# A hybrid decoder block on one Trainium2 core: small products of all lanes at every fourth step of the stream

## The chip, the cores and the metric

The kernel runs on one core of one Trainium2 chip. The metric is the device time of one execution in microseconds, as the median of several executions. Lower is better.

## The reference

One decoder layer for 512 tokens of width 2048 in float32, with an adaLN conditioning vector `c`. Cut to what matters:

```python
sh1, sc1, g1, sh2, sc2, g2 = split(silu(c) @ w_ada + b_ada)
h = rmsnorm(x, norm1_g) * (1 + sc1) + sh1
p = h @ w_in                                  # one projection, columns split
# A: convolution group: GLU, causal depthwise convolution of width 31, group norm, silu
u = p_val * sigmoid(p_gate);  u = conv31(u, conv_w) + conv_b
A = silu(group_norm(u, 16 groups))
# B: RWKV-7 group, 16 heads of 64: token shift, decay, a state update for every token
q = token_shift(p_rwkv);  r, k, v, xw, xa, xg = split(q)
S = S * w_t + (S a_t) b_t^T + v_t k_t^T;  y_t = S r_t
B = (group_norm(y) + bonus * v) * g           # bonus = sum(r * k * r_k)
x = x + g1 * (concat[A, B] @ w_out)
h = rmsnorm(x, norm2_g) * (1 + sc2) + sh2
x = x + g2 * ((silu(h @ w_ff1) * (h @ w_ff3)) @ w_ff2)
return rmsnorm(x, norm_f_g)
```

The output is (1, 512, 2048).

## The kernel before

Every large product runs as three products of split operands (`mm3`: high by high, high by low, low by high), 128 rows by 512 columns. After a head that projects the first columns, a **stream** (`stream`) walks over units of 16 steps; one step is one `mm3`. `in_units` are the projections in `ORDER`: k, v, r of pair 1, then for each pair of heads five units of 16 steps (val, gate of an earlier pair, k, v, r of the next), 592 steps in all. `out_units` are the output projection; its first 48 steps are the last ones beside which the lanes run, before `open_ff` at step 640 finishes what is left. While a step's products run, `emit` prepares the next weights: ScalarE copies the high part (line 92), VectorE subtracts for the low part (line 93).

Beside the stream run four **lanes** (class `Lane`). A lane has a queue of jobs, each a Python generator whose parts end at `yield`; the main loop calls `run` of every lane once after each step of the stream, and a list of numbers says how many steps the lane waits after each part.

- `pre` (`rwkv_pre`, 27 parts, one job per pair of heads): the decay and the keys (parts 1 to 6, with wide float32 products against `l1` and `bo`), the mask product `mp` (part 7), `vp` (8), `k` and `r` (8 to 10), the bonus product `bon` (11, its input is line 617), `npp` (12), two sets of transposes (13, 14), two `Q` products (15, 16), `nvp` (17), then the inverse of a triangular matrix. `inverse` takes the 16x16 diagonal blocks through DRAM to 64 lanes, where VectorE inverts them in 30 small operations (lines 701 and 704, spread over parts 12 to 16), brings them back through DRAM, and GpSimd spreads them (line 719, part 18); products follow in parts 19 to 23 (each with a VectorE or ScalarE read, line 736 among them), and parts 24 and 25 apply the inverse.
- `scan` (`rwkv_scan`, 20 parts): for each of eight chunks of 64 tokens a first half (64x64 products of the state, then `FV` on VectorE) and a second half (128x64 products, the new state), a chain of 16 parts; then a group norm (lines 812, 813, 818) and the split for the output projection.
- `cnv` (`conv`, 19 parts): 31 taps in 15 parts on VectorE (line 843), then a group norm with two wide products. Its input tile has one buffer: the convolution of the next pair needs the last one to be done (`cnv.finish` in `conv_gate`).
- `ada` (21 parts): 16 VectorE sums over loaded weights (line 882) and a product. Job 7 makes the gate row that `add_row` multiplies with the output projection's first sums; where it isn't there, `add_row` runs the lanes until it is.

The narrow products (64x64, 128x64, 64x128, 32x32) of the lanes are float32, eight to 32 instructions a part. PSUM has eight banks: three accumulators, `gg` (which the inverse's products and the mask product use), `yy` and `fp` for the scan, and two `bk` for everything that `aux` hands out. The tile framework orders each engine's queue and sets the waits.

Of the kernel before, what the change touches and what calls it, by code (L numbers as in the profile page):

```python
# [22 lines left out]
NB = CW // P  # L23
# [12 lines left out]
class Block:  # L36
    def __init__(self, ctx, tc, ins, out):
        self.ctx, self.tc, self.nc = ctx, tc, tc.nc
        self.i = ins
        self.out = out  # L40
        e = ctx.enter_context
        self.const = e(tc.tile_pool(name="const", bufs=1))
        self.act = e(tc.tile_pool(name="act", bufs=1))
        self.ps = e(tc.tile_pool(name="ps", bufs=1, space=PSUM))
        self.dram = e(tc.tile_pool(name="spill", bufs=1, space=DRAM))
# [170 lines left out]
    def fn(self, out, in_, func, **kw):  # L216
        name = self.SETS[func]
        nc, tc = self.nc, self.tc
        with ExitStack() as st:
            if self.last_fn is not None:  # L220
                st.enter_context(tc.issue_after(self.last_fn))
            if name != self.table:
                self.last_fn = nc.scalar.preload_act_table_set(name).ins
                self.table = name
            with tc.issue_after(self.last_fn):
                self.last_fn = nc.scalar.activation(out=out, in_=in_, func=func, **kw).ins  # L226
# [722 lines left out]
    def run(self):  # L949
# [20 lines left out]
        first = self.head()  # L970
# [6 lines left out]
        pres = []  # L977
        adas = [(3 + b // 4, b % 4, (sh2, s2)[b // 4], self.ada_cols) for b in range(8)]
        late = adas[8 - LATE:]
        adas = adas[:8 - LATE] + [(2, 0, None, self.ada_rows)]  # L980
        for n, ps in zip("rkv", first):
# [4 lines left out]
        pres.append((0, dict(self.rkv)))  # L986
        self.gate = {}
        ada = lambda part, cc, out, fn: fn(part, cc, out)
        self.scan, self.pre, self.cnv = Lane(self.scans, self.rwkv_scan, SCAN), Lane(pres, self.rwkv_pre, PRE, PRE0), \
            Lane(self.convs, self.conv, CONV)  # L990
        lanes = self.lanes = [self.scan, self.pre, self.cnv, Lane(adas, ada, ADA)]


        def in_units():
            last = ORDER[-1]
            for kind, b in ORDER:
                base = {"r": RWKV0, "k": RWKV0 + CW, "v": RWKV0 + 2 * CW, "val": 0, "gate": CW}[kind] + b * P

                def done(ps, kind=kind, b=b):
                    if kind in "rkv":  # L1000
                        self.rwkv_in(b, kind, ps)
                        if kind == "r":
                            pres.append((b, dict(self.rkv)))
                    elif kind == "val":
                        self.conv_val(b, ps)
                    else:
                        self.conv_gate(b, ps)
                stepped = None
                if (kind, b) == last:
                    def stepped(j):  # L1010
                        self.free += 1
                        self.mix_back(1)
                yield self.col_unit(i["w_in"][0], base, self.xh, self.xl, done, None, stepped)
# [35 lines left out]
        def out_units():  # L1049
            for cc in range(4):  # L1050
                accs = []
                for n, ks in enumerate(OUT_ORDER):
                    before = {(0, 3): open_ff, (1, 0): open_rows, (1, 1): lambda: load_x(1), (2, 0): lambda: load_x(2),
                              (3, 0): lambda: load_x(3)}.get((cc, n))
                    u = self.row_unit(
                        i["w_out"][0], ks, cc, self.mh, self.ml, accs, n == 0, n == 3,
                        self.add_row(2, cc, lambda t, cc=cc: self.x1[cc][:, t], rstd_rows),
                        before, (cc, n) == (3, 3))
                    if (cc, n) == (3, 3):
                        u.emit = {3: 1}  # L1060
                    yield u
# [272 lines left out]
        def units():  # L1334
            yield from in_units()
            yield from out_units()
            yield from fast_units()
            yield from ff2_units()

        for _ in self.stream(units()):  # L1340
            for l in lanes:
                l.run()

# [6 lines left out]

SCAN = (2, 2, 2, 3, 1, 1, 2, 3, 1, 1, 3, 2, 2, 2, 2, 2, 2, 1, 3, 2, 2)
PRE = (2, 2, 2, 2, 2, 2, 2, 2, 2, 2, 1, 2, 2, 2, 2, 3, 2, 8, 4, 2, 2, 2, 2, 1, 2, 2, 2, 1, 2)
CONV = (2, 2, 2, 2, 1, 2, 1, 2, 3, 3, 2, 2, 2, 2, 2, 2, 2, 3)
ADA = (4, 4, 4, 4, 4, 4, 4, 4, 4, 4, 4, 4, 4, 4, 4, 4, 4, 4, 6, 3, 3, 3)
ADA_ROWS = (2, 1, 2, 2, 2, 2, 2, 2, 3, 2, 3, 2, 2, 2, 2, 3, 2, 2, 4, 4, 2, 2)
PRE0 = PRE[:17] + (20,) + PRE[18:]  # L1360
LATE = 1
# [4 lines left out]
class Lane:  # L1366


    def __init__(self, queue, fn, waits, first=None):
        self.queue, self.fn, self.waits, self.first = queue, fn, waits, first or waits  # L1370
        self.job, self.n, self.wait, self.done = None, 0, 0, 0

    @property
    def busy(self):
        return bool(self.job or self.queue)

    def run(self):
        if self.wait:
            self.wait -= 1
        else:  # L1380
            next(self)

    def finish(self, n):

        while self.done < n:
            next(self)
# [129 lines left out]
```

## Time and profile before

| | us |
|---|---|
| median of 3 runs | 2484.78 (2482.81 to 2487.75) |
| the profiled execution | 2477.18 |
| its span, first to last instruction | 2475.5 |
| TensorE busy | 2373.9 (96%) |
| VectorE busy | 1784.8 (72%) |
| ScalarE busy | 1048.3 (42%) |
| mean granted TensorE clock | 0.984 |

Times in the profile are microseconds from the first instruction. PE is TensorE's products, PEld its weight loads, DVE is VectorE, ACT is ScalarE, POOL is GpSimd, SP is SyncE, which issues most transfers. A matmul's end is modelled, so what a product costs is read from the starts of the products around it. A float32 product is two instructions, a transpose and a stream product one. The stream's step 656 would start at about 931 us.

### The profile page before, as it was taken

What the parts mean: (1) busy time and instruction counts of PE and PEld (TensorE: products, weight loads), DVE (VectorE), ACT (ScalarE), POOL (GpSimd) and SP (SyncE); (2) the same over time, 40 slices, a digit from 0 to 9 for tenths busy, and PEclk for the clock granted to TensorE, in tenths of its full rate; (3) what the DMA queues carried; (4) which work ended last, traced back from release to release, by engine and by line L of the source; (5) the groups of instructions that cost most, each with busy time, mean ns of one, the idle gap of its engine ahead of it and who ended that gap; (6) DMA issues with size and microseconds to landing.
All of it is one profiled execution on the core that took longest, in us unless ns stands there. A gap on an engine that the chain in (4) does not pass through costs nothing. (4 is left out here: it accounts for less than half of the span.)

```text
span 2475.5 us, 36145 instructions
## 1 busy us (share of the span) xinstructions
PE 2373.9 (96%) x13984; PEld 1864.0 (75%) x13984; DVE 1784.8 (72%) x2727; ACT 1048.3 (42%) x1521; POOL 137.3 (6%) x232
## 2 busy tenths in 40 slices
PE   5998999999999998989999999999999999999998
PEld 4766667767766676767888888888888878888886
DVE  4764888888888885679878777787777867534434
ACT  4253464464454443246544444444444432222223
POOL 2000100100100100000000000000000000000000
PEclk9999999999999998999999999999999999999999
DMA  9953245344354458756777777767777886423332
GB/s 335 346 174 94 74 124 144 92 134 127 88 147 114 124 175 281 246 193 197 254 254 216 235 238 239 232 206 232 239 234 241 297 285 228 145 97 118 98 102 102
DMA packets 339372, 464.30 MB, mean 188 GB/s; under 512 B 42979, under 2 KB 165073, under 8 KB 338176
## 3 DMA queue, kind: packets, MB, share of 16 engines
q1 hardware_dynamic: 331312, 436.64, 56.7%
q0 software_dynamic: 7888, 25.36, 2.7%
q8 instruction: 109, 1.79, 0.3%
q14 instruction: 63, 0.52, 0.1%
HBM read 431.52 MB, written 30.41 MB: 187 GB/s over the span
## 5 line engine op out<-in xcount | busy, mean ns | idle before, releaser
L92 ACT CAST wh<-ws 128x512 fp32r<-128x512 f32 (+1 forms) x696 | 547.7, 810 | 888.8 <-PE acc L74 310.8
L93 DVE TENSOR_TENSOR wl<-ws,wh 128x512 fp32r<-128x512 f32 (+1 forms) x696 | 642.2, 938 | 364.9 <-ACT wh L92 360.5
L74 PE MATMUL acc<-xh,wh 128*128 128x512 f32 x592 | 258.7, 437 | 2.8 <-ACT wh L92 2.8
L74 PE MATMUL acc<-xl,wh 128*128 128x512 f32 x592 | 241.9, 409 | 0.0
L74 PE MATMUL acc<-xh,wl 128*128 128x512 f32 x592 | 238.6, 403 | 0.0
L882 DVE SCALAR_TENSOR_TENSOR ada<-wa,sc,ada 128x512 f32<-128x512 f32 x256 | 192.4, 752 | 63.6 <-DMA wa<-in_w_ada_dram 53.2
L74 PE MATMUL b<-wh,xh 128*128 128x512 f32 x560 | 222.1, 397 | 0.7 <-ACT ada L895 0.7
L74 PE MATMUL acc<-wh,xh 128*128 128x512 f32 x552 | 221.7, 402 | 0.0
L74 PE MATMUL acc<-wh,xl 128*128 128x512 f32 x552 | 219.7, 398 | 0.0
L74 PE MATMUL b<-wl,xh 128*128 128x512 f32 x560 | 219.6, 392 | 0.0
L74 PE MATMUL b<-wh,xl 128*128 128x512 f32 x560 | 219.1, 391 | 0.0
L74 PE MATMUL acc<-wl,xh 128*128 128x512 f32 x552 | 218.4, 396 | 0.0
L1453 DVE TENSOR_TENSOR ws<-ws,ws 128x1024 f32<-128x1024 f32 x123 | 149.7, 1217 | 0.0
L74 PEld LDWEIGHTS acc<-xh,wh 128*128 128x128 f32 x592 | 111.9, 189 | 35.6 <-issue 5.3
L74 PE MATMUL b<-wh,x 128*128 128x512 f32 x352 | 136.9, 389 | 1.4 <-ACT wh L92 1.4
L74 PE MATMUL b<-wl,x 128*128 128x512 f32 x352 | 137.0, 389 | 0.0
L74 PE MATMUL b<-wh,raw 128*128 128x512 f32 x352 | 137.0, 389 | 0.0
L74 PEld LDWEIGHTS acc<-xh,wl 128*128 128x128 f32 x592 | 112.5, 190 | 27.2 <-issue 2.2
L74 PEld LDWEIGHTS acc<-xl,wh 128*128 128x128 f32 x592 | 112.6, 190 | 24.5 <-issue 5.8
L74 PEld LDWEIGHTS b<-wh,xh 128*128 128x128 f32 x560 | 105.6, 189 | 24.1 <-ACT ada L895 2.2
L74 PEld LDWEIGHTS acc<-wl,xh 128*128 128x128 f32 x552 | 105.2, 190 | 23.8 <-DVE wl L93 2.3
L74 PEld LDWEIGHTS b<-wh,xl 128*128 128x128 f32 x560 | 105.8, 189 | 22.6 <-issue 0.5
(415 smaller groups left out, 4221.1 us busy)
## 6 DMA issues: line engine op xcount, KB each, us to landing
ws<-in_w_ff_dram SPq DMA_DIRECT2D x440, 512.0 KB, 4.8
wa<-in_w_ada_dram SPq DMA_DIRECT2D x256, 256.0 KB, 3.7
ws<-in_w_in_dram SPq DMA_DIRECT2D x74, 512.0 KB, 3.9
wa<-in_w_ada_dram SPq DMA_DIRECT2D x32, 1024.0 KB, 11.9
ws<-in_w_out_dram SPq DMA_DIRECT2D x24, 512.0 KB, 5.2
rawd<-wa POOLq DMA_DIRECT2D x28, 256.0 KB, 4.9
hr<-rawd POOLq DMA_DIRECT2D x7, 1024.0 KB, 6.3
hidd<-wa POOLq DMA_DIRECT2D x24, 256.0 KB, 5.3
```

Of the source, the lines that this page charges most:

```text
L74: return self.nc.tensor.matmul(out, lhsT=lhsT, rhs=rhs, start=start, stop=stop, skip_group_check=True)
L92: self.nc.scalar.copy(out=hi, in_=x)
L93: return self.nc.vector.tensor_tensor(out=lo, in0=x, in1=hi.bitcast(F32), op=ALU.subtract).ins
L882: nc.vector.scalar_tensor_tensor(out=acc, in0=was[r], scalar=self.sc[:, r:r + 1], in1=acc, op0=ALU.mult, op1=ALU.add)
L1453: k.nc.vector.tensor_tensor(out=out, in0=a, in1=b, op=ALU.subtract)
```

## The change

The main loop now tells each lane how many PSUM banks are free for small products at this step: two at every fourth step of the stream (`SLOT`), -1 at the others. While the first or the last pair is in preparation it is every second step. Each lane has a table (`SCAN_BANKS`, `PRE_BANKS`, `CONV_BANKS`, and `{20: 1}` for `ada`) with the banks that a part with small products takes; such a part (0 banks for those in `gg`, `fp` and `yy`) runs only where that many are left, in the order scan, pre, cnv, ada. A wait of 0 lets the lane go on with its next part at the same step. The lists of waits are new: the scan asks for every slot, so that a pair's chunks run beside the next pair's preparation; `PRE` puts parts 7 and 8, 12 and 13, 14 and 15, 16 and 17, 24 and 25 together and waits eight steps, where it was four, between GpSimd's spreading (part 18) and the inverse's products; convolutions wait three steps after each part, two at the end.

```diff
-        self.scan, self.pre, self.cnv = Lane(self.scans, self.rwkv_scan, SCAN), Lane(pres, self.rwkv_pre, PRE, PRE0), \
-            Lane(self.convs, self.conv, CONV)
-        lanes = self.lanes = [self.scan, self.pre, self.cnv, Lane(adas, ada, ADA)]
+        self.scan, self.pre, self.cnv = Lane(self.scans, self.rwkv_scan, SCAN, None, SCAN_BANKS), \
+            Lane(pres, self.rwkv_pre, PRE, PRE0, PRE_BANKS), Lane(self.convs, self.conv, CONV, None, CONV_BANKS)
+        lanes = self.lanes = [self.scan, self.pre, self.cnv, Lane(adas, ada, ADA, None, {20: 1})]
...
-        for _ in self.stream(units()):
+        for n, _ in enumerate(self.stream(units())):
+
+            ends = self.pre.done + bool(self.pre.job) in (1, NB)
+            if ends and self.pre.done:
+                self.cnv.waits = self.cnv.first = CONV_END
+            free = 2 if self.rowp is not None or n % (2 if ends else SLOT) == 0 else -1
             for l in lanes:
-                l.run()
+                free = l.run(free)
...
-SCAN = (2, 2, 2, 3, 1, 1, 2, 3, 1, 1, 3, 2, 2, 2, 2, 2, 2, 1, 3, 2, 2)
-PRE = (2, 2, 2, 2, 2, 2, 2, 2, 2, 2, 1, 2, 2, 2, 2, 3, 2, 8, 4, 2, 2, 2, 2, 1, 2, 2, 2, 1, 2)
-CONV = (2, 2, 2, 2, 1, 2, 1, 2, 3, 3, 2, 2, 2, 2, 2, 2, 2, 3)
+SLOT = 4
+SCAN = (1, 1, 1, 1, 1, 1, 1, 1, 1, 1, 1, 1, 1, 1, 1, 1, 2)
+PRE = (2, 2, 2, 2, 2, 2, 2, 0, 1, 1, 1, 6, 0, 2, 0, 2, 0, 8, 8, 2, 2, 2, 2, 2, 0, 1)
+CONV, CONV_END = (3,), (2,)
+
+SCAN_BANKS = dict.fromkeys(range(1, 16), 0) | {17: 1, 18: 1}
+PRE_BANKS = {1: 2, 2: 1, 7: 0, 8: 1, 11: 1, 12: 1, 13: 1, 14: 1, 15: 1, 16: 1, 17: 1} | dict.fromkeys(range(19, 24), 0) \
+    | {24: 1, 25: 1}
+CONV_BANKS = {16: 1, 17: 1}
 ADA = (4, 4, 4, 4, 4, 4, 4, 4, 4, 4, 4, 4, 4, 4, 4, 4, 4, 4, 6, 3, 3, 3)
...
-    def __init__(self, queue, fn, waits, first=None):
-        self.queue, self.fn, self.waits, self.first = queue, fn, waits, first or waits
+    def __init__(self, queue, fn, waits, first=None, banks={}):
+
+        self.queue, self.fn, self.waits, self.first, self.banks = queue, fn, waits, first or waits, banks
...
-    def run(self):
+    def run(self, free):
+
         if self.wait:
             self.wait -= 1
-        else:
+            return free
+        while True:
+            need = self.banks.get(self.n if self.job else 0)
+            if need is not None:
+                if need > free:
+                    return free
+                free -= need
             next(self)
+            if not self.job or self.wait >= 0:
+                self.wait = max(self.wait, 0)
+                return free
```

## Rows read from the trace of the kernel before

**Rows 1.** Windows: length, then each engine's busy time and instructions, granted clock, DMA.

```profile
233.00:833.00 600.00, 580.68 (x5225) 413.51 (x5219) 507.07 (x967) 308.86 (x467) 63.27 (x77) 1.00 0.41 115
931.00:941.00 10.00, 4.62 (x10) 1.34 (x8) 6.06 (x10) 6.56 (x9) 0.00 (x0) 0.78 0.87 286
```

**Rows 2.** TensorE's timeline around one set: start, busy, engine, line, out<-in, shape, count.

```profile
175.15 0.39 PE L74 MATMUL acc<-xh,wl 128*128 128x512 f32 x1
175.47 1.15 PE L74 MATMUL bk<-cen,v 64*64 64x64 f32 x32
176.55 0.50 PE L74 MATMUL acc<-xh,wh 128*128 128x512 f32 x1
176.89 0.39 PE L74 MATMUL acc<-xl,wh 128*128 128x512 f32 x1
```

**Rows 3.** TensorE's timeline around two sets side by side, 677 to 680 us.

```profile
676.84 0.40 PE L74 MATMUL acc<-xh,wh 128*128 128x512 f32 x1
677.08 0.39 PE L74 MATMUL acc<-xl,wh 128*128 128x512 f32 x1
...
679.45 0.50 PE L74 MATMUL acc<-xh,wl 128*128 128x512 f32 x1
679.79 0.39 PE L74 MATMUL acc<-xh,wh 128*128 128x512 f32 x1
```

**Rows 4.** TensorE's timeline, the last narrow products of the stage.

```profile
908.36 0.33 PE L74 MATMUL yy<-Q,FV 128*64 128x64 f32 x2
```

**Rows 5.** TensorE's timeline around one second half of a scan step.

```profile
694.42 0.40 PE L74 MATMUL acc<-xh,wl 128*128 128x512 f32 x1
694.74 0.33 PE L74 MATMUL yy<-Q,FV 128*64 128x64 f32 x2
695.00 0.49 PE L74 MATMUL acc<-xh,wh 128*128 128x512 f32 x1
695.42 0.34 PE L74 MATMUL fp<-FV,bkT 128*64 128x64 f32 x4
```

**Rows 6.** TensorE's timeline where two tile shapes adjoin, 322 to 325 us.

```profile
322.28 0.40 PE L74 MATMUL acc<-xl,wh 128*128 128x512 f32 x1
...
324.61 0.33 PE L74 MATMUL fp<-FV,bkT 128*64 128x64 f32 x2
324.87 0.50 PE L74 MATMUL acc<-xh,wl 128*128 128x512 f32 x1
325.21 0.40 PE L74 MATMUL acc<-xh,wh 128*128 128x512 f32 x1
```

**Rows 7.** Timeline of TensorE and VectorE at the end of the stage.

```profile
938.15 2.07 PE L74 MATMUL bk<-ada,ones 128*128 128x512 f32 x2 [3.28 <-DVE ada L882]
...
937.34 0.75 DVE L882 SCALAR_TENSOR_TENSOR ada<-wa,sc,ada 128x512 f32<-128x512 f32 x1 [1.23 <-DMA wa<-in_w_ada_dram]
938.01 0.74 DVE L859 SCALAR_TENSOR_TENSOR cy<-cy,colB,cu 128x512 f32<-128x512 f32 x1
```

**Rows 8.** TensorE's waits, 172 to 931 us: who for whom, us, times, longest.

```profile
PE bk L74 <- DVE r L617: 11.6, 7, 2.3
PE gg L74 <- POOL a L719: 8.3, 3, 5.7
PE gg L74 <- DVE a L736: 6.5, 5, 2.4
```

**Rows 9.** Timeline of VectorE and GpSimd between a mask product and a bonus product.

```profile
532.08 0.68 DVE L597 TENSOR_TENSOR kn<-gg,gm 128x512 f32<-128x512 f32 x1
...
533.34 1.76 DVE L93 TENSOR_TENSOR wl<-ws,wh 128x512 fp32r<-128x512 f32 x1
535.03 1.78 DVE L602 TENSOR_TENSOR k<-k,a 128x512 f32<-128x512 f32 x1
...
539.61 0.74 DVE L617 SCALAR_TENSOR_TENSOR r<-r,colB,k 128x512 f32<-128x512 f32 x1
...
532.91 1.65 POOL L682 TENSOR_TENSOR e<-kn,bd 128x512 f32<-128x512 f32 x1 [6.17 <-DVE kn L597]
```

**Rows 10.** Window after that bonus product.

```profile
540.60:544.00 3.40, 3.40 (x7) 1.82 (x6) 1.82 (x8) 0.00 (x0) 0.00 (x0) 0.50 0.61 193
```

## The prediction

> **What bounds the kernel now.** I read the windows by stage first [rows 1]. The stream's steps beside which the three large lanes run (640), and the 16 after them, end at about 931 us; in the long middle, 233 to 833 us, TensorE is busy 580.7 of 600 us and VectorE 507.1 (84.5%), so TensorE sets the pace and VectorE has 15% to spare. Between 931 and 941 us TensorE works 4.6 us only: it waits at the end of this stage. What follows has no lane left but the `ada` one, and the change leaves it alone.
>
> Then TensorE's own timeline. Two stream products next to each other start 0.23 us apart. One step of the preparation with 16 narrow products (32 instructions, 64x64) stretches the way from the stream product before it to the second one after it from 0.46 to 1.74 us [rows 2]: it costs 1.28 us. Two such steps that stand together, 64 instructions, cost 2.71 - 0.46 = 2.25 us [rows 3], not 2.56. So 32 instructions cost 0.97 us and 0.31 us is the price of going into narrow products and back, whatever their number. That price is what the change is about.
>
> I counted the stretches of narrow products along this timeline from 172 to 931 us: 250, the first in [rows 2], the last in [rows 4]; in 11 places a stretch changes its tile shape inside. 250 x 0.31 = 78 us of this stage go into and out of narrow products.
>
> **What moves.** No instruction is added or removed: the same products, vector operations and transfers, in another order. I stepped through the stream's loop with the old and the new lists (only the code is needed). Old: 240 lane steps with narrow products at 238 different steps of the stream. New: at 161, since each lane now waits for every fourth step (every second one for the first and last pair), and the preparation does two of its parts there at once (7 and 8, 12 and 13, 14 and 15, 16 and 17, 24 and 25). Inside these 161 stretches neighbours of the same shape meet 41 times and of another shape 38 times (a scan step's 128x64 beside the preparation's 64x64, the transposes' 64x128). Wide float32 products (the 512-column ones of `bo`, `cen`, `l1`, `l2`) run in the stream's own shape and are counted as a break; merging them is put at nothing.
>
> The trace's 250 is more than the code's 238, because the framework orders each engine's queue itself: second halves of scan steps are cut in two, two instructions, a stream product, then the rest [rows 5]. The first piece alone costs 0.58 - 0.23 = 0.35 us there. With four steps between a scan's halves the inputs are long there, and I expect no such cuts.
>
> **The sum.** (a) Up to the stream's step 560 (833.7 us) the trace has 220 stretches and 11 inner changes, the new order 140 and 38: 80 fewer stretches, 27 more inner changes. So 53 ways in and out vanish, 53 x 0.31 = 16.4 us, and 27 become a change of shape inside a stretch. What that saves lies between 0 and 0.31 us. In [rows 6] 60 recorded narrow instructions and two of 128x64 cost 2.93 - 0.46 = 2.47 us together; alone they would be 2.25 [rows 3] and 0.35 + 0.11 for the exit [rows 5, 2] = 0.46, so joining saved 0.24. I take the middle, 0.16: 27 x 0.16 = 4.3. Together **20.7 us**, ends 16.4 and 24.8.
>
> Here a rule of the Trainium skill speaks against the change: TensorEngine Tiling (Array Packing), Key Properties, says that a change of tiling mode, not just of tile, drains the engine. By it a change inside a stretch would cost as much as leaving it, and (a) would be its lower end; the 0.24 us of [rows 6] says not quite. It is a rival below.
>
> (b) After step 560 the old trace has 30 stretches, the new order 21: 9 x 0.31 = 2.8 us. I take **0**: this part ends on another chain. The convolution of the last pair but one starts only when its gate product is done (step 559), the last pair's only after that, and TensorE then waits at 931 us for VectorE: its product with the gate row starts at 938.15, 3.28 us idle, after the last `ada` sum (937.34) and beside the last convolution's scale at 938.01 [rows 7]. TensorE running faster here just waits longer. Gains before step 560 do carry over, since they bring the gate product forward.
>
> (c) The inverse. TensorE waits 8.3 us for GpSimd's diagonal blocks (3 times, the longest 5.7) and 6.5 us for VectorE's additions between the inverse's products (5 times, the longest 2.4) [rows 8]. Part 18 now waits eight steps, not four, and parts 19 to 23 stand four steps apart, not two. The 5.7 us belongs to the first pair, whose part 19 moves by one step (51 to 52) while three merges bring TensorE there earlier: it stays. One wait of about 2.4 belongs to the last pair, where slots are two steps apart: it stays. The rest goes, 2.6 + 4.1 = **6.7 us**. What is late next there is nothing: the next pair's preparation waits for its inputs.
>
> (d) The bonus product. TensorE waits 11.6 us in 7 places for line 617 [rows 8]. In [rows 9] VectorE reads the mask's product at 532.08 and ends line 617 at 540.35: 8.3 us, with operations of 1.76 and 1.78 us where the same kind takes 0.68, while GpSimd works from 532.91 on. Three operations in between are the former pair's closing ones (lines 813, 818 and 93), some 0.7 us each as the unstretched ones of [rows 9], so 2.1 us; in the new order they stand forty steps away. But the way for TensorE shrinks as well: part 7 and the bonus now stand one slot apart (steps 388 and 392, before 381 and 388): about 1.0 us of `vp`, four steps at 0.69 and one scan half at 8 x 0.03 + 0.31 = 0.55, 4.3 us, against 6.2 us of VectorE's work. A wait of some 1.9 us per pair against 1.7 now: **0**, ends -11.6 (the queue is free) and +12 us (one stretched operation more, 1.76 us, in each of 7 pairs).
>
> (e) The `ada` lane's last part now needs a slot with a free bank and runs after the other lanes. Job by job it falls behind; job 7, the gate row on which the out projection's first sum waits, begins at step 603, not 588, and parts 14 to 17 are then forced at step 652. Its loads go out on SyncE's queue that much later, behind the stream's weights. The sums end the stage [rows 7]; four are left over, each with its 0.75 us and at most the wait for its load of 1.23 that the last one shows, so the loss is between 0 and 4 x 1.98 = 7.9 us; most of it hides beside the last convolution, which ends at the same time: **2 us** lost.
>
> Other moves cost nothing that I can find: a scan takes 68 steps instead of 37, under the next pair's preparation, and ends (pair 4: step 438) before the pair after it begins (447); a preparation ends at 445 instead of 426, two steps before the next starts, which is the tightest of these margins; convolutions are paced at three steps and still end some 40 steps before their buffer is wanted; the last scan ends at step 622 (624 before), the last convolution at 628 (630).
>
> 20.7 + 6.7 - 2 = 25.4 us. The profiled execution took 2477.2 us (span 2475.5), so 2451.8; the median of the runs shown is 7.6 us above it, 2484.8, and I forecast 2484.8 - 25.4 = **2459**.
>
> **The rivals.** *Slower: the bonus wait grows.* The point is 25.4 / 7 = 3.6 us more per pair. If VectorE still needs its 8.3 us and one stretched split of 1.76 on top [rows 9] in a window of 4.3, each pair waits 5.8 us, 4.1 more than now; and TensorE standing that long would fall to half clock, as after the wait for line 617 that ended at 540.35, where from 540.6 to 544 the granted clock is 0.50 and seven products come in 3.4 us [rows 10], 1.7 us lost. 7 x 5.8 = 41 us against the gain of 25: 16 slower, 2500. For it: the operations stretched beside GpSimd stay. Against: the closing operations leave. Chance 0.15. *VectorE becomes the bound.* Its 507 us in 600 become 507 in 575, 88%, and as its queue is in order each burst at a slot arrives late; half of the gain is lost: 2472. Chance 0.15. *A change of shape inside a stretch costs a full way out and in*: (a) is 16.4, the time 2463; against it stands the 0.24 us of [rows 6], for it that this is one place. Chance 0.13. (This is what the rule of the Trainium skill named above, TensorEngine Tiling (Array Packing), Key Properties, would give.) *It doesn't do what it says*: the framework's order pulls the parts of a slot apart again, as [rows 5] shows that it may; then only (c) and (e) are left, 4.7 us: 2480. Chance 0.08. The forecast itself 0.49.
>
> **How the numbers follow.** Best bounds of all terms: 24.8 + 2.8 + 6.7 + 11.6 + 1.7 (the half clock of [rows 10] gone) = 48 us, 2437. Above, the range takes in three of the four rivals and leaves out the slower one: 2482. A difference under 0.2% (5 us) can't be told from no change. Faster: nearly all of the forecast, the shape change and VectorE as bound, and half of the pulled-apart case, 0.78; slower 0.15; same 0.07.
>
> **What would show it.** In the new profile: TensorE's narrow products in about 160 stretches, scan halves beside preparation products, and no second half cut in two; the price of a shape change inside a stretch, read as in [rows 6]; waits for lines 719 and 736 down to the first and the last pair; waits for line 617 near 1.7 us each (over 5 would be the slower rival); VectorE's share in the middle near 88%; 931 us moved to about 904, and behind it a stall like the one in [rows 7], up to some us longer. I am wrong if the count stays above 220, if the bonus wait doubles, or if TensorE waits at slots for bank evacuations.

## The result, and the profile after

The changed kernel takes **2455.3 us** (2453.6 to 2458.5) against 2483.8 (2476.4 to 2487.8) for the kernel before, measured beside it: the ratio is **0.9896**, interval 0.9879 to 0.9913. The forecast was 2459, range 2437 to 2482. The profiled execution took 2455.66 us (span 2453.8); its clock is 0.984, as before. A later measurement, beside the last three experiments and with a second profile, gave 2455.6 and 0.9899 (0.9881 to 0.9917). Below, "before" and "after" name the two kernels.

The two windows that answer to [rows 1] (length, then busy time and instructions of PE, PEld, DVE, ACT, POOL, granted clock, DMA share, GB/s): the same 600 us of the middle, and from the end of the stream's step 656 to its restart.

```profile
205.00:805.00 600.00, 578.72 (x5479) 427.94 (x5478) 496.18 (x972) 311.55 (x473) 66.40 (x81) 1.00 0.42 118
908.50:920.50 12.00, 5.28 (x9) 1.45 (x7) 6.27 (x10) 6.38 (x9) 0.00 (x0) 0.65 0.60 200
```

TensorE is as busy as before, with 5% more instructions in the same 600 us; VectorE is at 83%, where it was 84.5% (88% forecast). The end of the stage moved from 931 to 908.5 us, and the hole behind it grew from 9.8 to 12.0 us.

**The account.** I cut every trace at three marks that are the same stream product in each: the start of steps 16 and 560, and of a step 716, which is 60 steps behind the stage's end and so behind the hole. These names, here, above and in the expectations, are four too high: by the order of the products in the trace they are steps 12, 556 and 712, and the hole stands ahead of step 652, not 656 (ScalarE reads the gate product of step 559 at 838.53 us in before, not ahead of 833.95). They mean the same product in every trace, so the differences stand. "Own time" is the length less the waits and less half of the time at the lower clock, 1.2 GHz; that halving is too much where TensorE also waits, so own time is best compared between traces with little of it. Stretches are counted along TensorE's timeline.

| kernel | 16 to 560 | waits | at half clock | stretches + inner changes of shape | own time | 560 to 716 | behind 716 | span |
|---|---|---|---|---|---|---|---|---|
| before | 661.3 | 26.8 | 10.2 | 220 + 11 | 629.4 | 156.1 | 1485.5 | 2475.5 |
| after | 635.6 | 25.4 | 6.8 | 163 + 38 | 606.8 | 163.8 | 1484.7 | 2453.8 |
| after, second profile | 640.7 | 26.9 | 13.7 | 163 + 38 | 606.9 | 161.0 | 1484.2 | 2454.1 |

The stage up to step 560 gives 25.7 us (20.6 in the second profile), of which TensorE's own time makes 22.6 (22.5 there). The waits are as long as before. Behind step 560 the new kernel loses 7.7 us (4.9). The rest of the difference of the spans, 3.0 us (4.5), lies ahead of step 16, where the time at half clock was 20.5 us in before and 13.7 in both profiles of after; another kernel with the change has 20.5 there again, so I do not count it as the change's.

**What a stretch costs now.** TensorE's timeline in after (start, busy, engine, line, out<-in, tile, shape, count): a second half of a scan step alone; the same beside two sets of 64x64; a half, the eight transposes and a set, three shapes; a scan's first half and two sets of the preparation, all 64x64.

```profile
331.66 0.39 PE L74 MATMUL acc<-xh,wl 128*128 128x512 f32 x1
331.98 0.34 PE L74 MATMUL fp<-FV,bkT 128*64 128x64 f32 x4
...
332.70 0.39 PE L74 MATMUL acc<-xl,wh 128*128 128x512 f32 x1
...
338.32 0.39 PE L74 MATMUL acc<-xh,wl 128*128 128x512 f32 x1
338.63 0.34 PE L74 MATMUL fp<-FV,bkT 128*64 128x64 f32 x4
...
339.02 0.97 PE L74 MATMUL gg<-ar,bk 64*64 64x64 f32 x26
...
341.20 0.40 PE L74 MATMUL acc<-xl,wh 128*128 128x512 f32 x1
...
357.16 0.39 PE L74 MATMUL acc<-xh,wl 128*128 128x512 f32 x1
...
359.92 0.39 PE L74 MATMUL acc<-xl,wh 128*128 128x512 f32 x1
...
362.21 0.39 PE L74 MATMUL acc<-xh,wl 128*128 128x512 f32 x1
362.53 0.28 PE L74 MATMUL fp<-S,ar 64*64 64x64 f32 x2
...
363.63 0.22 PE L74 MATMUL bk<-FV,e 64*64 64x64 f32 x1
363.63 0.22 PE L74 MATMUL bk<-ar,bk 64*64 64x64 f32 x1
...
364.94 0.39 PE L74 MATMUL acc<-xl,wh 128*128 128x512 f32 x1
```

Read as in [rows 2]: from the stream product before the stretch to the second one after it, less 0.46. The half alone costs 332.70 - 331.66 - 0.46 = 0.58 us. Two sets alone cost 2.25 [rows 3]. Half and two sets together cost 2.42, not 2.83: the joint saves **0.41**, across a change of shape. Eight scan products and two sets of one shape cost 2.27, the sets alone nearly as much. A first half alone costs 0.57 (334.99 to 336.02), so it has all but vanished: **0.55** saved. The joint with the transposes saves less. Eight of them alone cost 0.83 in before (829.97 to 831.26), a set 1.28, a half 0.58, together 2.69; side by side they cost 359.92 - 357.16 - 0.46 = 2.30, so two joints save 0.39, **0.20** each. What a joint saves depends on which shapes meet.

**Waits.** The largest of TensorE's waits from 172 to 905 us, which answer to [rows 8] (us in all, times, longest):

```profile
PE fp L74 <- DVE S L792: 8.1, 7, 2.3
PE gg L74 <- POOL a L719: 6.8, 5, 1.9
PE gg L74 <- DVE a L736: 2.8, 2, 2.6
PE bk L74 <- DVE r L617: 2.1, 3, 0.9
```

Lines 719, 736 and 617 had 26.4 us, now 11.7. What they gave, a wait of the scan took (0.8 us in before), with smaller ones. At its longest, VectorE and then TensorE:

```profile
544.97 0.44 DVE L701 TENSOR_TENSOR tmp<-xl,lane 64x169 f32<-64x169 f32 x1
545.34 0.74 DVE L843 SCALAR_TENSOR_TENSOR cy<-cu,colC,cy 128x512 f32<-128x512 f32 x1
546.00 0.32 DVE L704 TENSOR_REDUCE xl<-tmp 64x13 f32<-64x169 f32 x1
546.24 0.73 DVE L843 SCALAR_TENSOR_TENSOR cy<-cu,colD,cy 128x512 f32<-128x512 f32 x1
...
547.30 0.27 DVE L792 SCALAR_TENSOR_TENSOR S<-fp,pc,Sp 128x64 f32<-128x64 f32 x1
...
547.62 0.33 PE L74 MATMUL fp<-S,ar 64*64 64x64 f32 x4 [2.26 <-DVE S L792]
```

The convolution's taps (line 843) and the inverse's small operations (701, 704) stand ahead of the scan's new state (792) in VectorE's queue, and the scan's next half, due at its slot, waits 2.26 us for 0.27 us of work.

**The end of the stage**, which answers to [rows 7]: TensorE, VectorE, ScalarE.

```profile
910.64 1.12 PE L74 MATMUL bk<-cy,cen 128*128 128x512 f32 x2 [1.77 <-DVE cy L843]
913.20 2.05 PE L74 MATMUL bk<-cu,bo 128*128 128x512 f32 x2 [1.43 <-ACT cu L852]
915.03 1.91 PE L74 MATMUL bk<-ada,ones 128*128 128x512 f32 x2
920.47 0.80 PE L74 MATMUL b<-wh,xh 128*128 128x512 f32 x1 [3.52 <-ACT ada L895]
...
909.85 0.74 DVE L843 SCALAR_TENSOR_TENSOR cy<-cu,colD,cy 128x512 f32<-128x512 f32 x1
913.95 0.75 DVE L882 SCALAR_TENSOR_TENSOR ada<-wa,sc,ada 128x512 f32<-128x512 f32 x1 [0.65 <-DMA wa<-in_w_ada_dram]
...
919.22 0.72 ACT L226 ACTIVATE cy<-cy,colB 128x512 f32<-128x512 f32 x1
919.85 0.56 ACT L895 COPY ada<-bk 128x512 f32<-128x512 f32 x1
```

The `ada` sums no longer end the stage. The last tap ends at 910.6, the convolution's two wide products and its functions on ScalarE follow (with two loads of function tables there, at 915.99 and 917.93, of 1.28 us each), and the gate row's copy (919.85), though its product started at 915.03, stands behind them in ScalarE's queue.

### The profile page after: what moved, and what is told of

Same layout as the page of the kernel before. It is cut to its first block, busy times and chain, and to the rows that moved or that the text cites. A ratio compares the mean times of both kernels' runs of the same rounds, so it can differ in the third digit from the quotient of the medians.

```text
span 2453.8 us, 36133 instructions
## 1 busy us (share of the span) xinstructions
PE 2351.2 (96%) x13984; PEld 1863.1 (76%) x13984; DVE 1767.9 (72%) x2727; ACT 1049.5 (43%) x1521; POOL 138.4 (6%) x232
## 5 line engine op out<-in xcount | busy, mean ns | idle before, releaser
L74 PEld LDWEIGHTS b<-wh,xh 128*128 128x128 f32 x560 | 105.6, 189 | 26.8 <-ACT ada L895 5.1
```

What stands on the lines that cost most here:

```text
L74: return self.nc.tensor.matmul(out, lhsT=lhsT, rhs=rhs, start=start, stop=stop, skip_group_check=True)
```

## The experiments

**Where the gain sits.** *The spacing alone:* the kernel before with eight steps ahead of the inverse's products.

```diff
-PRE = (..., 2, 8, 4, 2, 2, 2, 2, 1, 2, 2, 2, 1, 2)
+PRE = (..., 2, 8, 8, 2, 2, 2, 2, 1, 2, 2, 2, 1, 2)
```

> The kernel before with one number changed: part 18 of the preparation waits eight steps, not four, before the inverse's products. If the wait for GpSimd's blocks outside the first pair (2.6 of 8.3 us) is worth its length, 2 to 4 us faster than before, and that wait is down to the first pair's. If waits of this kind only move to the next product, no change. If the change's whole gain of about 22 us (span 2475.5 to 2453.8) were spacing, most of it would be here.

2487.0 us, ratio 1.0031 (1.0018 to 1.0045): a little slower. The waits for the inverse, TensorE's from 172 to 940 us, and the longest stretch at half clock with the wait before it:

```profile
PE gg L74 <- DVE a L736: 16.6, 5, 3.8
PE gg L74 <- POOL a L719: 10.7, 3, 5.8
...
774.92 1.98 PE L74 MATMUL gg<-pi,e 64*64 64x64 f32 x32 [2.91 <-DVE a L736]
...
773.90:791.00 17.10, 16.08 (x127) 12.05 (x127) 9.41 (x16) 1.86 (x4) 0.53 (x1) 0.50 0.20 57
```

Both waits grew ([rows 8]: 6.5 and 8.3), and behind them TensorE ran 47.8 us at half clock up to step 560, 10.2 in before. Four more steps alone don't hide GpSimd's spreading in the old order.

*The spacing taken out of the new order:* after, with four steps there.

```diff
-PRE = (..., 0, 8, 8, 2, 2, 2, 2, 2, 0, 1)
+PRE = (..., 0, 8, 4, 2, 2, 2, 2, 2, 0, 1)
```

> The kernel after, with four steps in place of eight between the preparation's part 18 and part 19 (one slot): the named spacing of the change alone undone. Theory A (the eight steps hide GpSimd's spreading): TensorE's waits for line 719 rise from 6.8 us to 10 or more, with a few us of half clock behind them: 2459 to 2466. Rival B (as the spacing alone on the kernel before, first run: waits change their place, the sum stays): 2453 to 2458.

2460.0 us, ratio 0.9926 (0.9910 to 0.9942). The wait in question, TensorE's from 168 to 906 us:

```profile
PE gg L74 <- POOL a L719: 14.4, 7, 3.7
```

Theory A: twice the 6.8 us of after, and half clock up to step 560 at 17.1 us. Against 0.9896 and 0.9899 the spacing is worth some 7 us in the new order (the intervals still touch). It pays beside the slots and not without them.

*The lanes kept apart:* after, the scan at steps 0, 4, 8 ... and the other lanes two steps later, so that a chunk never stands beside the next pair's preparation, except for the first and last pair.

```diff
-            for l in lanes:
-                free = l.run(free)
+            if ends or len(lanes) < 4 or self.rowp is not None:
+                for l in lanes:
+                    free = l.run(free)
+            else:
+                lanes[0].run(free)
+                free = 2 if n % SLOT == 2 else -1
+                for l in lanes[1:]:
+                    free = l.run(free)
```

> The changed kernel, but the scan has the steps 0, 4, 8, ... and all other lanes 2, 6, 10, ..., so that scan products no longer stand beside the preparation's; lists and spacing stay. By the code 196 stretches of narrow products where the changed kernel has 161. If the ways in and out of narrow products are what was gained, 35 more stretches with 19 fewer inner changes of shape cost 16 x 0.31 + 19 x (0.16 to 0.3) = 8 to 11 us: about a third to a half of the gain is lost. If the gain is shorter waits, which this leaves alone, the time of the changed kernel within 2 us.

2452.9 us, ratio 0.9895 (0.9874 to 0.9916), the same as after. 189 + 18 stretches in place of 163 + 38, and own time 616.0 us, 9.2 more; but the waits up to step 560 fall to 17.8 us, 7.6 less, the scan's among them (TensorE's from 168 to 906 us):

```profile
PE gg L74 <- POOL a L719: 3.9, 5, 1.7
PE fp L74 <- DVE S L792: 3.6, 3, 2.8
```

So the chunks beside the next pair's preparation save about what I thought a joint saves, and cost the same again in waits: VectorE gets the reads of both lanes at one slot. What is left as the source of the net gain is the preparation's own parts put together, the even grid and the spacing. That is by elimination: only the spacing was taken out alone, and how much each of the other two gives is not shown.

**The waits.** *The bonus product later in the old order*, four steps in place of one ahead of it.

```diff
-PRE = (2, 2, 2, 2, 2, 2, 2, 2, 2, 2, 1, 2, ...)
+PRE = (2, 2, 2, 2, 2, 2, 2, 2, 2, 2, 4, 2, ...)
```

> The kernel before with one number changed: the bonus product (part 11) comes four steps after line 617's part, not one. If the 11.6 us that TensorE waits for line 617 are on the path, 10 to 13 us faster than before (11.6 and the half clock at 540.6, 1.7). If the wait only moves to the products behind it, or the lost time is made up before the end of the stage, under 4 us.

2482.9 us, ratio 1.0012 (0.9995 to 1.0029): no difference, although the wait of [rows 8] for line 617, 11.6 us, is gone. The wait for line 736 rose from 6.5 to 14.0 us, that for 719 from 8.3 to 11.7, the time at half clock from 10.2 to 34.1. A wait that is taken from one place of this chain turns up at the next.

*The convolutions later*, after, their taps held back 16 steps, then at a pace of two, so that they leave the inverse's small operations.

```diff
-            if ends and self.pre.done:
+            if ends and self.pre.done > 1:
-CONV, CONV_END = (3,), (2,)
+CONV, CONV_END = (16, 2), (2,)
```

> The changed kernel, but the convolutions of the first six pairs start 16 steps later, after the preparation's parts 12 to 17. In the changed kernel TensorE newly waits 8.1 us for the scan's state (line 792), which VectorE reaches late because convolution taps alternate with the inverse's 30 small operations. If that is the cause, this wait is under 3 us and the time 4 to 8 us below the changed kernel. If the state is late because VectorE stands at the transfer of the diagonal blocks (18.0 us in 6 places), the wait stays and the time is that of the changed kernel within 2 us.

2463.4 us, ratio 0.9934 (0.9913 to 0.9956), slower than after. The two waits that changed most, TensorE's from 168 to 906 us:

```profile
PE gg L74 <- POOL a L719: 16.2, 8, 4.1
PE fp L74 <- DVE S L792: 2.2, 5, 0.9
```

The wait for S fell from 8.1 to 2.2 us, as it should if the taps crowd it; GpSimd's blocks now come late instead, 6.8 to 16.2, and the time at half clock rose from 6.8 to 23.9.

*The written pace.* In after the list that gives the convolutions a pace of three never counts: the condition for the end also holds between the first and the second preparation, near step 63, and sets the pace of two for good. This run lets the list count.

```diff
-            if ends and self.pre.done:
+            if ends and self.pre.done > 1:
```

> The kernel after, but the convolutions keep the pace of three that the list CONV gives, until the last pair is in preparation; in the kernel after they run at two from the second one on, because the condition for the end also holds once near step 63. Theory A (taps at a pace of two crowd VectorE where the inverse's small operations stand): TensorE's wait for the scan's S (line 792) falls from 8.1 us to 3 to 5, GpSimd's blocks stay near 6.8, the time is 2450 to 2453. Rival B (as with the late convolutions of the fourth run: the crowding moves to another place): S falls, but the waits for GpSimd's blocks rise to 10 or more, time 2456 to 2462.

2452.4 us, ratio 0.9898 (0.9880 to 0.9916): the time of after. The waits moved as the rival said (S 2.4 us, line 719 16.4), but ten stretches fewer (153 + 35) paid for it, own time 600.9. The pace makes no difference to the time. The own times line up with the count: 220, 189, 163 and 153 stretches (before, the lanes apart, after, this run) have 629.4, 616.0, 606.8 and 600.9 us, the last the least sure, with 20.5 us at half clock.

**The end of the stage.** *The `ada` lane's slot:* after, the lane's last part no longer waits for a free bank.

```diff
-Lane(adas, ada, ADA, None, {20: 1})
+Lane(adas, ada, ADA, None, {})
```

> The kernel after, but the ada lane's last part (its product with the ones) no longer waits for a slot with a free bank. My step (e) said that this gate makes the lane late and costs 2 us at the end of the stage (bounds 0 and 7.9). Theory A (step (e)): about 2 us faster than the kernel after, 2453 against 2455.3, and the 12.0 us between the end of step 656 and the restart of the stream shrink to about 10. Rival B (the gate costs nothing: the last sums end well before the last convolution's scale): 2455 within 1.5, and the 12.0 us stay.

2454.3 us, ratio 0.9905 (0.9886 to 0.9923): no difference. The hole shrank from 12.0 to 10.2 us, but steps 560 to 716 take 164.1 us, as in after (163.8). The gate costs nothing that can be measured.

*The last convolutions faster:* after, at a pace of one from the last pair's preparation on.

```diff
-                self.cnv.waits = self.cnv.first = CONV_END
+                self.cnv.waits = self.cnv.first = CONV_END if self.pre.done == 1 else (1,)
```

> The kernel after, with the last convolutions at a pace of one, not two, from the last pair's preparation on. Theory A (the taps of the last convolutions are what VectorE still has to do when TensorE stands at the end of the stage): the 12.0 us from the end of step 656 to the restart fall to 9 or 10, and the 103.2 us from step 560 to the end fall by up to 3: 2450. Rival B (taps at twice the pace crowd the last pair's inverse): the waits for lines 719 and 736 between steps 560 and 600 rise by 3 us or more, with half clock: 2457 to 2461.

2457.8 us, ratio 0.9919 (0.9904 to 0.9934), no gain and perhaps some us lost; steps 560 to 716 rose to 170.8. The crowding came, but not where the rival had it: the last scan fell behind. Its norm now stands after the end of step 656.

```profile
917.20 1.02 PE L74 MATMUL bk<-f,bo 128*128 128x512 f32 x2
...
925.75 2.04 PE L74 MATMUL bk<-ada,ones 128*128 128x512 f32 x2 [5.63 <-ACT f L226]
```

*Less for VectorE:* after, with half of the last two convolutions' taps left out.

```diff
-            v.scalar_tensor_tensor(out=y, in0=u[:, t:t + T], scalar=self.tap(t, b), in1=y,
-                                   op0=ALU.mult, op1=ALU.add)
+            if t < 16 or b < 6:
+                v.scalar_tensor_tensor(out=y, in0=u[:, t:t + T], scalar=self.tap(t, b), in1=y,
+                                       op0=ALU.mult, op1=ALU.add)
```

> The kernel after, with the last 15 of the 30 VectorE taps left out in the convolutions of the last two pairs (30 operations, 30 x 0.66 = 20 us of VectorE's work between step 560 and the end of the stage). In the kernel after that stretch, step 560 to the restart of the stream, takes 115.2 us, of which VectorE is busy 91.7. Theory A (VectorE's work sets the end of the stage; that is where the gain made before step 560 is partly given back): the stretch falls to 100 to 106 us, the time is 10 to 14 us below the kernel after. Rival B (the end is set by the chain from the last gate product through the inverse and by TensorE's own work): the stretch falls by 2 to 3 us, the time by 2 to 3.

2440.9 us, ratio 0.9848 (0.9826 to 0.9871), 14.7 us below after on the same chip. The window from step 560 to step 716 in after (its second profile), then here:

```profile
808.90:969.90 161.00, 148.36 (x910) 109.48 (x909) 118.38 (x200) 61.16 (x97) 7.13 (x10) 0.94 0.61 201
```

```profile
805.90:957.90 152.00, 143.11 (x910) 107.02 (x909) 100.82 (x173) 61.44 (x97) 6.88 (x10) 0.98 0.65 215
```

17.6 us of VectorE's work less make this part 9.0 us shorter, and here nothing is lost behind it (1481.3 for 1484.2): theory A, the part ends on VectorE. Of the 14.7 us these 9.0 are the part's; the others, 2.7 ahead of it and 2.9 behind, have no cause that the run shows. The kernel before has nearly the same work there (115.5 us), and the last convolution's taps can't start before the gate product of step 591. So what TensorE gains in this part it waits out at its end.

*The sums earlier:* after, with the `ada` lane at a pace of three, so that the last 16 sums are done in the middle of the stage.

```diff
-ADA = (4, 4, 4, 4, 4, 4, 4, 4, 4, 4, 4, 4, 4, 4, 4, 4, 4, 4, 6, 3, 3, 3)
+ADA = (3,)
```

> The kernel after, with the ada lane at a pace of three steps, not four, so that its 16 last sums (12.1 us of VectorE's work, now between step 560 and the end of the stage) are done in the middle of the stage. Theory A (VectorE's work sets the end): the 115.2 us from step 560 to the restart fall by 6 to 10, the middle gets 1 to 3 us slower, and the time is 4 to 8 us below the kernel after. Rival B (the end is set by the convolutions' taps alone, which can't start before the gate products of steps 559 and 591): the stretch falls by 1 to 2 us, the middle loses as much, same time within 2 us. Rival C (VectorE in the middle, busy 83% of it, has no room): the waits there rise from 25 to 30 us or more, 4 us or more slower.

2459.6 us, ratio 0.9919 (0.9901 to 0.9936), 4 above after. Theory A holds in its place and fails in the sum: steps 560 to 716 fall from 161.0 to 143.3 us, the hole is gone, the middle is as long as in after's second profile (639.9 for 640.7), and behind step 716 everything is lost again, 1499.8 in place of 1484.2. There the output projection needs the next gate rows, whose sums now wait for their loads (TensorE, then VectorE):

```profile
962.65 2.08 PE L74 MATMUL gg<-ada,ones 128*128 128x512 f32 x2 [6.57 <-DVE ada L882]
...
961.85 0.75 DVE L882 SCALAR_TENSOR_TENSOR ada<-wa,sc,ada 128x512 f32<-128x512 f32 x1 [2.29 <-DMA wa<-in_w_ada_dram]
...
954.60:1014.00 59.40, 47.32 (x186) 36.89 (x185) 33.36 (x51) 12.99 (x26) 3.22 (x6) 0.89 0.84 273
```

From 954.6 to 1014 us the transfers are busy 84% of the time and TensorE 47.3 of 59.4 us.

*Both, with the pace of three:* after, with the edits of the last run and of the one on the written pace together.

> The last one with the convolutions at the written pace of three as well. If both effects stand by themselves (theory A there, and the fewer stretches of the pace of three: 153 in place of 163, 600.9 us of TensorE's own work up to step 560 in place of 606.8), this is the fastest of all, 2443 to 2449. Rival: its taps and sums meet VectorE's small operations of the inverse, GpSimd's blocks are waited for 16 us as with the pace of three alone, and the time is that of the kernel after or above.

2459.5 us, ratio 0.9922 (0.9900 to 0.9945): the rival. Line 719 is waited for 16.5 us, half clock up to step 560 is 27.3, and the part behind step 716 is long too, 1494.9.

*After itself* beside the last three is the second measurement of the first section.

> The kernel after itself, beside the next three on the same chip, so that they are compared with it and not by way of two ratios. Every theory expects 0.9896 of the kernel before, some 2452 to 2456.

No version that does all of the work was faster than the changed kernel by more than can be told.

## Why the prediction came out right, and where it didn't

The time is 3.7 us below the forecast; between the profiled executions the difference is 21.5 us, between the medians 28.5 and, in the later measurement, 24.1, against 25.4 forecast. The mechanism was right: fewer ways into narrow products and back shorten TensorE's own time. That the sum fits so well is luck, since its terms met it by errors that cancel. Between the two profiles 22.6 us of own time, 1.4 of waits and 1.7 of half clock are gained, 7.7 are lost behind step 560, and the 3.7 left, ahead of step 16 and behind step 716, I don't count as the change's.

- **(a) The stretches: right in sum, wrong in both factors.** 20.7 us forecast, 22.6 found in TensorE's own time. I expected 80 stretches fewer and found 57 (220 to 163): the step that failed is "I expect no such cuts". Up to step 560 nine pieces of two second-half products stand alone in after, 13 in before. Seven cut second halves and five sets in two pieces make up 12 of the 23 stretches above the code's 140; the rest are mostly parts of one slot that came apart, with stream products between them. One cut half, as in [rows 5]:

```profile
380.50 0.33 PE L74 MATMUL yy<-Q,FV 128*64 128x64 f32 x2 [0.18 <-DVE FV L780]
380.76 0.50 PE L74 MATMUL acc<-xh,wh 128*128 128x512 f32 x1
381.19 0.34 PE L74 MATMUL fp<-FV,bkT 128*64 128x64 f32 x4
```

 The price was too low: 0.31 for a joint of one shape, where the timeline shows 0.55 for eight scan products beside two sets, and 0.16 for one across shapes, where it shows 0.41 for a scan half and 0.20 with transposes. I had measured the first at two equal sets and halved the second between its ends; [rows 6], 0.24 in one place, was the nearest row and I went below it. With the counts as found my prices would give 30 x 0.31 + 27 x 0.16 = 13.6 us, and 0.55 and 0.41 everywhere 27.6; the 22.6 lies between, as a mix of joints should.
- **The rule on the change of shape.** The Trainium skill's TensorEngine Tiling (Array Packing), Key Properties, says that a change of mode drains the engine. These traces show a price for the change below that of leaving the narrow products: joining across shapes saved 0.41 of the half's 0.58 us, and 0.20 a joint with the transposes. That rival would have made (a) 16.4 (30 x 0.31 = 9.3 with the counts found); it is 22.6.
- **(b) After step 560: the reason right, the size wrong.** The part does end on VectorE, as the run with half of the taps shows, and TensorE's gain there is lost. But it is not the 0 I put: steps 560 to 716 are 4.9 to 7.7 us longer, with waits of 12.6 and 12.7 us for 9.9 and half clock of 20.5 and 27.3 us for 17.1. 28 stretches stand there, not 21.
- **(e) The `ada` lane: wrong.** I held its sums for the end of the stage and charged 2 us for their slot. In after they end before the last convolution does, and without the slot the time is the same.
- **(c) The inverse: 5.2 of 6.7 us.** Lines 719 and 736 went from 14.8 to 9.6 us. The sum nearly fits by luck: the 5.7 us of the first pair, which I said would stay, are 1.9 at most, and where I had the other waits for line 719 (2.6 us) going to nothing there are now 6.8 us in five places. Line 736 went as forecast: 0.2 us are left up to step 560, and 2.6 for the last pair. The eight steps are needed: with four the wait for 719 alone is 14.4.
- **(d) The bonus product: wrong.** I put 0 and a rival of 16 us slower; the wait went from 11.6 to 2.1 us. The window for TensorE is some 4.0 us (4.3 forecast; from the last mask product at 426.13 to the bonus product at 430.13), but VectorE needs 3.0, not 6.2. Its queue from the mask's product on, and GpSimd's operation beside it:

```profile
426.57 0.68 DVE L597 TENSOR_TENSOR kn<-gg,gm 128x512 f32<-128x512 f32 x1
427.18 0.68 DVE L613 TENSOR_TENSOR bk<-k,pi 128x512 f32<-128x512 f32 x1
427.77 1.78 DVE L617 SCALAR_TENSOR_TENSOR r<-r,colB,k 128x512 f32<-128x512 f32 x1
...
427.40 1.61 POOL L682 TENSOR_TENSOR e<-kn,bd 128x512 f32<-128x512 f32 x1 [4.65 <-DVE kn L597]
```

 The stretched operation is there, as the rival had it, but the split of a weight and line 602 stand ahead of the mask's product, not behind it as in [rows 9]: I took the old queue, less the closing operations, into the new order.
- **The wait I didn't see.** (c) and (d) together gave back 14.7 us, and up to step 560 TensorE still waits as long as before. The scan at every slot meets VectorE's taps and the inverse's operations; the run with the lanes apart has 17.8 us of waits in place of 25.4. "VectorE becomes the bound" was the right rival in kind: not by its busy share, which was 83% and no higher than before, but by the order of its queue at the slots.
- **The pace of three** in my reading of the lists was wrong, and without effect on the time.

## What to carry to other kernels

Count how often TensorE goes into small tiles and back, and price it per stretch from the timeline: here some 0.4 us for each of 57 stretches gone (22.6 us), and a joint saves more where the shapes are the same (0.55) than across them (0.41 and 0.20). But bringing the lanes together brings their reads to VectorE together as well: price the queue of the engine that must answer at a slot, operation by operation in the new order, not by its busy share. And where a stage ends on another engine (here VectorE's taps), or the next stage on its loads, a gain ahead of it is kept only as far as it brings that work forward too.

## What the runs showed of the hardware

- **Eight small products came free beside 64 of the same shape.** In the stretch at 362 us the 72 cost 2.27 us where 64 cost 2.25 [rows 3], and four others like it in after cost 2.15 to 2.27; the framework had mixed the parts' instructions, and two of different parts are recorded with the same start, 363.63. The Trainium skill, TensorEngine Tiling (Array Packing), Key Properties, says that different tiles can execute matmuls in parallel. The rows agree with it but don't prove it, since a product's end is modelled.
- **The clock falls behind the same wait in one execution and not in another.** In both profiles of after the scan waits for line 792 at 547.6 us, for 2.26 and 1.95 us. The window behind it, after first, then its second profile:

```profile
548.30:555.10 6.80, 6.80 (x39) 5.19 (x38) 6.70 (x14) 1.78 (x3) 1.66 (x4) 1.00 0.34 52
```

```profile
548.30:555.10 6.80, 6.80 (x21) 5.63 (x22) 6.04 (x12) 1.69 (x3) 0.89 (x3) 0.50 0.17 33
```

 One keeps 1.00, the other runs at 0.50 for 6.8 us with TensorE busy throughout, and TensorE does about half as many instructions (21 for 39). So a wait costs its own length and, at times, some us behind it; up to step 560 the kernels have between 6.8 and 47.8 us of it, the most in the one with the longest waits for line 736. Over 23 executions of before the time goes from 2466.8 us at a mean clock of 0.987 to 2486.4 at 0.981.
